# A two-layer decoder trunk: the second layer's input scaling and the low parts of keys and queries, moved from VectorE to GpSimd

## The chip, the core and the metric

The kernel runs on one core of a Trainium2 chip. The time is device microseconds for one execution; the kernel before has a median of 788.73 us in three runs (788.3 to 789.17). In the profile PE is TensorE (PEld its weight loads), DVE is VectorE, ACT is ScalarE, POOL is GpSimd and SP issues most of the DMAs. A line such as L573 is a line of the kernel before, unless the text says otherwise; in the changed kernel the lines from 850 on have a number one higher.

## What is computed

There are 528 tokens (16 meta tokens and 512 of input), width 1024, and two layers. In each, one projection of the normed residual feeds a pooling mixer and a latent attention with eight heads, and gates join the two:

```python
h = rmsnorm(h_res, norm_gain[l])
proj = h @ w_in[l]
u_pool, z_pool, c_q, c_kv, k_rope, z_mla, g_pool, g_mla = jnp.split(proj, IN_SPLIT_POINTS, axis=-1)
y_pool = (pool_mix(u_pool, pool_w_group[l], pool_scale[l]) * jax.nn.silu(z_pool)) @ pool_w_up[l]
...
q = rmsnorm(q, g_qn)
k = rmsnorm(k, g_kn)
...
o = causal_block_attention(q, k, v)
...
merged = jax.nn.sigmoid(g_pool) * y_pool + jax.nn.sigmoid(g_mla) * y_mla
h_res = h_res + merged @ w_out[l]
```

## The kernel before

**Split products.** Every float32 product is made of three matmuls on rounded parts (`mm3`, L188, L191, L192): high weight by high input, high weight by low input, low weight by high input. A part pair comes from two steps: ScalarE copies the value into the rounded type (hi), and VectorE subtracts that from the value (lo). For weights the steps are L183 (`whi`) and L184 (`wlo`), 263 times; for data `split` (L295, L296).

**A stream and its fillers.** All projections form one list of weight chunks of 512 columns, and a generator issues them one after the other. The attention takes steps of that stream to fill the time between its own matmuls (`fill_now`, `fill`, `fill_to`). The framework then orders each engine's instructions by its own timeline of the program, so the order in the code is not quite the order on an engine.

**Layer 2 around the change.** After the query statistics (`qk_stats`) the loop over `renorm` scales the eight input tiles by the norm factor, `inv`, and by the gain, and splits them into `hh` and `hl`; tiles 4 to 7 come first, then 0 to 3, and tiles 0 to 3 are loaded again (L571). Each product is held behind a matmul of the stream. On the same VectorE queue run the Newton steps for the query norm (L303 to L309) and the sums and differences of `mixed` (L583 to L586). Meanwhile PE runs `pu`, which does not need the renormed input; `zm0` and `zm1` behind it are the first that do.

**The heads.** `prep(h)` makes head h's keys and queries: keys times a factor, one half on VectorE (L847), the other on GpSimd (L848), then the parts `kh` and `kl`; queries into `qh` and `ql` (L854, L855), with rotary rows by DMA (L858). Two heads' parts are held at once. `head(h)` makes the scores `S`, the masked extremes (L877), the exponentials (L884), and on GpSimd the products with the reciprocal sums (L922, L924, eight for a head). `prep(h + 1)` follows `head(h)` in the code.

Of the kernel before, what the change touches and what calls it, by code (L numbers as in the profile page):

```python
# [9 lines left out]
F32 = mybir.dt.float32  # L10
# [3 lines left out]
AF = mybir.ActivationFunctionType  # L14
ALU = mybir.AluOpType
# [7 lines left out]
NM = 16  # L23
T = SEQ + NM
# [25 lines left out]
G_H, G_CKV, G_CQ, G_QN, G_QR, G_KN, G_KR, G_PS = 0, 8, 10, 16, 17, 18, 19, 20  # L50
# [22 lines left out]
def trunk(ctx, tc, xT, pos, win, wkr, wqb, wkb, wvb, wgr, wpu, wmu, wout, gains, const, yT):  # L73
    nc = tc.nc
    pe, act, dve, gp, sp = nc.tensor, nc.scalar, nc.vector, nc.gpsimd, nc.sync
# [15 lines left out]
    def slot(tag, dt=F32, bufs=1, w=W):  # L91
        return sl.tile([P, w], dt, tag=tag, name=nm(tag), bufs=bufs)

    def tmp(w=W):
        return tp.tile([P, w], F32, tag="tmp", name=nm("tmp"), bufs=3)
# [104 lines left out]
    newest = [None]  # L200
# [90 lines left out]
        while clk[0] < end and step():  # L291
            pass

    def split(hi, lo, src, a, b):
        act.activation(hi[:, a:b], src, AF.Copy)  # L295
        dve.tensor_sub(lo[:, a:b], src, hi[:, a:b].bitcast(F32))  # L296

    def behind(ins, other):
        tc.add_manual_dep(ins.ins, other.ins.name,
                          mybir.DependencyInfo(mybir.DependencyClass.Sync, mybir.DependencyReason.DATA))  # L300
# [56 lines left out]
    class Layer:  # L357
# [208 lines left out]
        def renorm(self, k):  # L566
            assert k < 4 or (self.l, f"pu{k}") not in done
            f = self.f[k] = slot("sv", bufs=2) if k % 4 == 3 else slot(f"cq{k}")
            f, (hh, hl), x = f[:, NM:T], self.hs[k], xb[:, k, NM:T]
            if k < 4:  # L570
                sp.dma_start(f, scr[:, k, :])  # L571
                x = f
            behind(dve.scalar_tensor_tensor(out=f, in0=x, scalar=self.g(G_H + k), in1=self.inv[:, NM:T],  # L573
                                            op0=ALU.mult, op1=ALU.mult), newest[0])
            split(hh, hl, f, NM, T)

        def mixed(self, i):
            k, s = divmod(i, 2)
            if k > 3 or not self.last:
                return  # L580
            u, w = self.f[k], self.f[k + 4]
            if s == 0:
                dve.tensor_sub(w[:, b:c], u[:, b:c], w[:, b:c])  # L583
                dve.tensor_sub(u[:, b:c], u[:, a:b], u[:, b:c])
                dve.tensor_sub(u[:, a:b], u[:, a:b], w[:, b:c])
                dve.tensor_sub(w[:, a:b], w[:, a:b], u[:, a:b])  # L586
                return
            if k == 0:
                self.half = [sqt().bitcast(F32R) for _ in range(14)]
                spare = slot("rinv", F32R)  # L590
                self.half += [spare[:, 0:HALF], spare[:, HALF:T]]
            th, tl = (slot(f"cq{(3, 0, 1, 2)[k] + j}", F32R) for j in (0, 4))
            t3h, t3l, t4h, t4l = (t[:, :N2] for t in self.half[4 * k:4 * k + 4])
            split(th, tl, u[:, a:c], a, c)
            for h_, l_, v in ((t3h, t3l, w[:, b:c]), (t4h, t4l, w[:, a:b])):
                split(h_, l_, v, 0, N2)
            self.tt[k] = {6: (th[:, a:b], tl[:, a:b]), 5: (th[:, b:c], tl[:, b:c]), 7: (t3h, t3l), 4: (t4h, t4l)}
# [242 lines left out]
        def prep(self, h):  # L840
            p, odd = h // 2, h % 2
            n0, r0 = (64, 0) if odd else (0, 64)
            kf = tmp()
            bc = self.bcs.pop(h)
            if h + 2 < H:
                self.spread_k(h + 2)
            dve.tensor_mul(kf[n0:n0 + 64, :], self.kn[p][n0:n0 + 64, :], bc[n0:n0 + 64, :])  # L847
            gp.tensor_mul(kf[r0:r0 + 64, :], self.kp[r0:r0 + 64, :], bc[r0:r0 + 64, :])  # L848
            kh, kl = slot("kh", F32R, bufs=2), slot("kl", F32R, bufs=2)
            split(kh, kl, kf[:, :T], 0, T)  # L850
            qh, ql = qhl[odd]
            x0 = self.x0
            src = self.qn[p][n0:n0 + 64, x0:T]
            act.activation(qh[n0:n0 + 64, x0:T], src, AF.Copy)  # L854
            dve.tensor_sub(ql[n0:n0 + 64, x0:T], src, qh[n0:n0 + 64, x0:T].bitcast(F32))  # L855
            g0 = 32 * (h % 4)
            for d, f in zip((qh, ql), self.qr[h // 4]):
                sp.dma_start(d[r0:r0 + 32, x0:T].bitcast(F32), f[g0:g0 + 32, x0:T].bitcast(F32))  # L858
            return kh, kl, qh, ql
# [433 lines left out]
```

## Time and profile before

| | |
|---|---|
| median of three runs | 788.73 us |
| the profiled execution | 788.28 us |
| its span | 786.4 us |
| PE busy | 778.8 us |
| DVE busy | 558.8 us |
| ACT busy | 427.1 us |
| POOL busy | 210.9 us |

PE's ends are modelled and its matmuls overlap, so a busy PE may still lose a little; the starts of two matmuls show it better. The groups give a line, engine, operation, the tiles, the shapes and the count, then the busy time, the mean in ns, and the idle time just before with what ended it. Timeline rows give the start, the duration, and the same names. Rows of stretches give busy time by engine.

### The profile page before, as it was taken

How to read it: one execution, taken by the hardware profiler on the slowest of the kernel's cores; microseconds unless marked ns; L12 is line 12 of the kernel's file. 1: busy time of each engine (PE TensorE's matmuls, PEld its weight loads, DVE VectorE, ACT ScalarE, POOL GpSimd, SP SyncE). 2: the span in 40 equal slices, each digit the busy share in tenths (PEclk: the TensorE clock that was granted, in tenths of full speed). 3: DMA queues.
4: the chain of work that ended last, by engine and by line, in shares of the span. 5: the costliest groups of instructions: out<-in, count | busy, mean ns of one | idle time of the engine just before them, and what ended most of it. 6: DMA issues, size and time to landing. Idle time of an engine off the chain costs nothing.

```text
span 786.4 us, 15094 instructions
## 1 busy us (share of the span) xinstructions
PE 778.8 (99%) x5445; PEld 713.4 (91%) x5445; DVE 558.8 (71%) x1229; ACT 427.1 (54%) x974; POOL 210.9 (27%) x275
## 2 busy tenths in 40 slices
PE   9999999999999999999999999999999999999998
PEld 8999899999999999999997898887778999887887
DVE  5848778447788977685355487775897899874932
ACT  8545655635656665643354455556657676654421
POOL 1034504002434342153000145122004323440600
PEclk9999999999999999999999999999999999999999
DMA  6242343434645435647742422435233454462372
GB/s 243 82 101 84 99 120 102 128 106 117 136 122 126 116 90 112 167 103 176 206 141 81 109 81 79 138 97 167 95 111 112 118 153 126 121 202 68 99 231 100
DMA packets 60907, 97.61 MB, mean 124 GB/s; under 512 B 9744, under 2 KB 18320, under 8 KB 60832
## 3 DMA queue, kind: packets, MB, share of 16 engines
q1 hardware_dynamic: 57520, 90.61, 38.8%
q0 software_dynamic: 2304, 4.20, 4.3%
q10 hardware_dynamic: 1008, 1.84, 0.7%
q8 instruction: 43, 0.70, 0.4%
q14 instruction: 32, 0.26, 0.1%
HBM read 88.64 MB, written 14.23 MB: 131 GB/s over the span
## 4 chain that ended last, share of the span: by engine, by line
PE 91%; DVE 4%; DMA 2%; issue 1%; ACT 1%; ACTq 0%; DVEq 0%
PE mm L188 27%; PE mm L192 27%; PE mm L191 26%; PE mm L944 2%; PE S L191 2%; PE S L192 2%; PE S L188 1%; DVE wlo L184 1%; PE o L950 1%; PE o L949 1%; PE S L498 1%; PE mm L400 1%; DMA xb<-xT 1%; DMA raw<-win 1%; DVE hl L296 0%
## 5 line engine op out<-in xcount | busy, mean ns | idle before, releaser
L188 PE MATMUL mm<-hh,whi 128*128 128x264 f32 (+2 forms) x1080 | 333.9, 311 | 0.1
L191 PE MATMUL mm<-hl,whi 128*128 128x264 f32 (+2 forms) x1080 | 332.5, 309 | 0.4 <-DVE hl L296 0.4
L192 PE MATMUL mm<-hh,wlo 128*128 128x264 f32 (+2 forms) x1080 | 332.1, 310 | 0.4 <-DVE wlo L184 0.4
L184 DVE TENSOR_TENSOR wlo<-raw,whi 128x512 fp32r<-128x512 f32 (+2 forms) x263 | 197.7, 756 | 108.8 <-ACT whi L183 105.3
L183 ACT ACTIVATE whi<-raw 128x512 fp32r<-128x512 f32 (+2 forms) x263 | 157.8, 603 | 179.3 <-PE mm L191 114.6
L188 PEld LDWEIGHTS mm<-hh,whi 128*128 128x128 f32 x1080 | 202.9, 188 | 11.8 <-ACT racc L958 0.5
L191 PEld LDWEIGHTS mm<-hl,whi 128*128 128x128 f32 x1080 | 203.3, 188 | 11.1 <-DVE hl L296 0.9
L192 PEld LDWEIGHTS mm<-hh,wlo 128*128 128x128 f32 x1080 | 202.5, 188 | 10.5 <-DVE wlo L184 1.1
L700 POOL TENSOR_TENSOR racc<-racc,tmp 128x264 f32<-128x264 f32 (+1 forms) x15 | 14.2, 950 | 144.2 <-ACT tmp L699 119.8
L192 PE MATMUL mm<-cq,wlo 128*128 128x264 f32 (+2 forms) x140 | 43.5, 313 | 0.6 <-DVE wlo L184 0.6
L188 PE MATMUL mm<-cq,whi 128*128 128x264 f32 (+2 forms) x140 | 44.0, 314 | 0.0
L191 PE MATMUL mm<-cq,whi 128*128 128x264 f32 (+2 forms) x140 | 43.4, 311 | 0.0
L848 POOL TENSOR_TENSOR tmp<-kp,bc 64x528 f32<-64x528 f32 x16 | 23.7, 1484 | 68.5 <-PE mm L815 44.4
L1049 POOL TENSOR_TENSOR tmp<-tmp,xb 128x264 f32<-128x264 f32 (+1 forms) x24 | 27.2, 1155 | 50.4 <-DVE tmp L1047 38.9
L877 DVE CUSTOM_DVE_ANT_0 S<-S,maskw,nqs 128x288 f32<-128x288 f32 (+4 forms) x80 | 38.3, 497 | 3.0 <-PE S L192 2.8
L922 POOL TENSOR_TENSOR pm<-pa,rs 128x16 f32<-128x16 f32 x32 | 10.9, 340 | 96.7 <-DVE rs L917 88.6
L188 PE MATMUL mm<-u,whi 128*128 128x264 f32 (+1 forms) x108 | 35.2, 326 | 0.1
L296 DVE TENSOR_TENSOR tl<-mm,th 128x512 fp32r<-128x512 f32 (+1 forms) x64 | 29.4, 481 | 7.7 <-ACT th L295 6.5
L192 PE MATMUL mm<-u,wlo 128*128 128x264 f32 (+1 forms) x108 | 34.7, 322 | 0.0
L924 POOL TENSOR_TENSOR cq<-cq,rs 128x384 f32<-128x384 f32 (+1 forms) x32 | 32.8, 1024 | 0.0
L191 PE MATMUL mm<-kn,whi 128*128 128x264 f32 (+1 forms) x96 | 30.6, 320 | 0.0
L188 PE MATMUL mm<-q,whi 128*128 128x264 f32 (+1 forms) x96 | 29.9, 323 | 0.6 <-ACT q L295 0.4
(309 smaller groups left out, 1472.3 us busy)
## 6 DMA issues: line engine op xcount, KB each, us to landing
raw<-win SPq DMA_DIRECT2D x139, 256.0 KB, 2.7
raw<-wout SPq DMA_DIRECT2D x32, 256.0 KB, 3.3
bc<-kdr SPq DMA_DIRECT2D x16, 264.0 KB, 4.1
raw<-wpu SPq DMA_DIRECT2D x16, 256.0 KB, 2.8
wsum<-win SPq DMA_DIRECT2D x16, 256.0 KB, 3.3
raw<-wmu SPq DMA_DIRECT2D x16, 256.0 KB, 2.8
raw<-wsum SPq DMA_DIRECT2D x16, 256.0 KB, 3.2
raw<-wqb SPq DMA_DIRECT2D x12, 256.0 KB, 2.6
```

The source lines that it names most:

```text
L183: act.activation(hi[:, :n], raw[:, :n], AF.Copy)
L184: dve.tensor_sub(lo[:, :n], raw[:, :n], hi[:, :n].bitcast(F32))
L188: first = pe.matmul(out, wh, xh, start=start, stop=False, skip_group_check=more)
L191: pe.matmul(out, wh, xl, start=False, stop=False, skip_group_check=more)
L192: newest[0] = pe.matmul(out, wl, xh, start=False, stop=stop, skip_group_check=more)
L296: dve.tensor_sub(lo[:, a:b], src, hi[:, a:b].bitcast(F32))
L700: self.acc_last = gp.tensor_add(self.acc[:, a:b], self.acc[:, a:b], t[:, :b - a])
L848: gp.tensor_mul(kf[r0:r0 + 64, :], self.kp[r0:r0 + 64, :], bc[r0:r0 + 64, :])
L877: dve.tensor_tensor_reduce(out=sv, in0=sv, in1=mask, scale=nqs[:, i, h:h + 1], scalar=3e38, op0=ALU.add, op1=ALU.min, accum_out=bia[:, c:c ...
L924: gp.tensor_mul(pt[i][:, NM:], pt[i][:, NM:], rs[:, i:i + 1].to_broadcast([P, n - NM]))
L944: pe.transpose(tr[:, P * (i - j):P * (i - j + 1)], pt[i][:, NM + P * j:NM + P * (j + 1)], ident)
L1049: gp.tensor_add(t[:, :b - a], t[:, :b - a], self.am[m][:, a:b])
```

## The change

In layer 2 `renorm` multiplies the tile by `inv` on GpSimd, and a ScalarE pass in place applies the gain; before, one VectorE instruction did both. In `prep`, the subtractions that make `kl` and `ql` run on GpSimd in layer 2 and on VectorE in layer 1 as before. Nothing else is changed, and the result is the same quantity.

```diff
-    def split(hi, lo, src, a, b):
+    def split(hi, lo, src, a, b, eng=dve):
         act.activation(hi[:, a:b], src, AF.Copy)
-        dve.tensor_sub(lo[:, a:b], src, hi[:, a:b].bitcast(F32))
+        eng.tensor_sub(lo[:, a:b], src, hi[:, a:b].bitcast(F32))
...
-            behind(dve.scalar_tensor_tensor(out=f, in0=x, scalar=self.g(G_H + k), in1=self.inv[:, NM:T],
-                                            op0=ALU.mult, op1=ALU.mult), newest[0])
+            behind(gp.tensor_mul(f, x, self.inv[:, NM:T]), newest[0])
+            act.activation(f, f, AF.Copy, scale=self.g(G_H + k))
             split(hh, hl, f, NM, T)
...
-            split(kh, kl, kf[:, :T], 0, T)
+            rest = gp if self.last else dve
+            split(kh, kl, kf[:, :T], 0, T, rest)
...
-            dve.tensor_sub(ql[n0:n0 + 64, x0:T], src, qh[n0:n0 + 64, x0:T].bitcast(F32))
+            rest.tensor_sub(ql[n0:n0 + 64, x0:T], src, qh[n0:n0 + 64, x0:T].bitcast(F32))
```

The framework orders each engine anew. GpSimd in layer 2, from the last rotary step of the queries on, in the kernel before (`kp` is the keys' rotary part, `pm` and `pa` belong to head 0's softmax):

```order
L533 TENSOR_TENSOR q_1328_7177<-q_1328_7177,tmp_7183 128x512
L848 TENSOR_TENSOR tmp_7574<-kp_6423,bc_6912 64x528
L848 TENSOR_TENSOR tmp_7761<-kp_6423,bc_6914 64x528
L922 TENSOR_TENSOR pm_7706<-pa_7613,rs_7617 128x16
L924 TENSOR_TENSOR pa_7613<-pa_7613,rs_7617 128x128
```

The same place behind the change (L856 makes ql, L296 kl, L573 the renorm's products; `cq`, `sv` are the renormed tiles, 4 to 7 and then 0 to 3):

```order
L856 TENSOR_TENSOR qhl_106<-q_1339_7221,qhl_105 64x512
L856 TENSOR_TENSOR qhl_108<-q_1339_7221,qhl_107 64x512
L848 TENSOR_TENSOR tmp_7582<-kp_6423,bc_6912 64x528
L573 TENSOR_TENSOR cq_1390_7438<-xb,rinv_6066 128x512
L296 TENSOR_TENSOR kl_7588<-tmp_7582,kh_7587 128x528
L573 TENSOR_TENSOR cq_1395_7463<-xb,rinv_6066 128x512
L573 TENSOR_TENSOR cq_1396_7475<-xb,rinv_6066 128x512
L573 TENSOR_TENSOR sv_7493<-xb,rinv_6066 128x512
L573 TENSOR_TENSOR cq_1402_7505<-cq_1402_7505,rinv_6066 128x512
L573 TENSOR_TENSOR cq_1407_7524<-cq_1407_7524,rinv_6066 128x512
L573 TENSOR_TENSOR cq_1412_7550<-cq_1412_7550,rinv_6066 128x512
L573 TENSOR_TENSOR sv_7563<-sv_7563,rinv_6066 128x512
```

Two products for keys have become twelve operations before the second of them: two ql, kf0, eight renorm products and head 0's kl, which is second among these nine.

VectorE in the renorm stretch before, up to the hl of tile 2 (`hl_11_133`), the last rows of 34 from the first L573:

```order
L573 SCALAR_TENSOR_TENSOR cq_1412_7544<-cq_1412_7544,gn,rinv_6066 128x512
L296 TENSOR_TENSOR hl_9_131<-cq_1407_7519,hh_8_130 128x512
L296 TENSOR_TENSOR sq_7739<-cq_1390_7438,sq_7738 128x256
L584 TENSOR_TENSOR cq_1402_7501<-cq_1402_7501 128x256
L308 TENSOR_TENSOR nt_7419<-nt_7419,na_7417 128x40
L573 SCALAR_TENSOR_TENSOR sv_7556<-sv_7556,gn,rinv_6066 128x512
L184 TENSOR_TENSOR wlo_7597<-raw_7594,whi_7596 128x512
L583 TENSOR_TENSOR cq_1396_7473<-cq_1412_7544,cq_1396_7473 128x256
L584 TENSOR_TENSOR cq_1407_7519<-cq_1407_7519 128x256
L296 TENSOR_TENSOR hl_11_133<-cq_1412_7544,hh_10_132 128x512
```

Behind the change, the last rows of 38 from the first weight split of that stretch to the same hl:

```order
L296 TENSOR_TENSOR hl_9_131<-cq_1407_7524,hh_8_130 128x512
L184 TENSOR_TENSOR wlo_7605<-raw_7602,whi_7604 128x512
L585 TENSOR_TENSOR cq_1402_7505<-cq_1402_7505,cq_1390_7438 128x256
L584 TENSOR_TENSOR cq_1407_7524<-cq_1407_7524 128x256
L583 TENSOR_TENSOR cq_1396_7475<-cq_1412_7550,cq_1396_7475 128x256
L586 TENSOR_TENSOR cq_1390_7438<-cq_1390_7438,cq_1402_7505 128x256
L583 TENSOR_TENSOR sv_7493<-sv_7563,sv_7493 128x256
L585 TENSOR_TENSOR cq_1407_7524<-cq_1407_7524,cq_1395_7463 128x256
L184 TENSOR_TENSOR wlo_7645<-raw_7642,whi_7644 128x512
L296 TENSOR_TENSOR hl_11_133<-cq_1412_7550,hh_10_132 128x512
```

The L573 rows are gone; more of the sums (L583, L585, L586) and a second weight split (`wlo_7645`) stand ahead of this hl, and the whole Newton chain, of which five rows stood ahead of it, is done before them.

GpSimd at head 5 before (`tmp_8700` is its key product, the L922 and L924 rows head 4's softmax):

```order
L848 TENSOR_TENSOR tmp_8700<-kp_6423,bc_8171 64x528
L922 TENSOR_TENSOR pm_8635<-pa_8483,rs_8487 128x16
L924 TENSOR_TENSOR pa_8483<-pa_8483,rs_8487 128x128
...
L924 TENSOR_TENSOR cq_1637_8485<-cq_1637_8485,rs_8487 128x512
L922 TENSOR_TENSOR pm_8635<-pa_8750,rs_8754 128x16
```

Behind the change:

```order
L856 TENSOR_TENSOR qhl_106<-q_1369_7332,qhl_105 64x512
L848 TENSOR_TENSOR tmp_8708<-kp_6423,bc_8179 64x528
L923 TENSOR_TENSOR pm_8643<-pa_8491,rs_8495 128x16
...
L925 TENSOR_TENSOR cq_1637_8493<-cq_1637_8493,rs_8495 128x512
L296 TENSOR_TENSOR kl_8714<-tmp_8708,kh_8713 128x528
L856 TENSOR_TENSOR qhl_108<-q_1369_7332,qhl_107 64x512
L923 TENSOR_TENSOR pm_8643<-pa_8758,rs_8762 128x16
```

Head 5's kl (`kl_8714`) now stands behind all eight of head 4's softmax products; head 2's stands so behind head 1's.

## The prediction

> **What bounds the kernel now.** I read the page first, then the busy time by stretch, then the waits of the matmul engine, then the instructions of the stretch the change touches.
>
> ```profile
> span 786.4 us, 15094 instructions
> PE 778.8 (99%) x5445; PEld 713.4 (91%) x5445; DVE 558.8 (71%) x1229; ACT 427.1 (54%) x974; POOL 210.9 (27%) x275
> PE 91%; DVE 4%; DMA 2%; issue 1%; ACT 1%; ACTq 0%; DVEq 0%
> ```
>
> The matmul engine is busy nearly always and holds 91% of the chain that ended last. A change beside it can win only what it waits for now, and loses whatever new wait it makes. The change lies in layer 2 only: the renorm stretch (about 553 to 575 us) and the eight heads (575 to 690 us).
>
> ```profile
> 550.00:575.00 25.00, 24.15 (x124) 18.06 (x120) 22.89 (x49) 14.18 (x28) 1.52 (x1) 1.00 0.31 96
> 575.00:600.00 25.00, 25.00 (x124) 21.11 (x123) 23.03 (x61) 15.95 (x40) 5.56 (x9) 1.00 0.34 106
> 600.00:690.00 90.00, 89.10 (x620) 82.17 (x620) 81.25 (x197) 64.03 (x167) 33.43 (x51) 1.00 0.43 127
> PE mm L192 <- DVE wlo L184: 1.0, 2, 0.6
> PE o L949 <- DVE tmp L965: 0.5, 1, 0.5
> PE mm L191 <- DVE hl L296: 0.4, 1, 0.4
> PE mm L188 <- DVE sv L625: 0.3, 1, 0.3
> ```
>
> The columns are stretch, its length, then PE, PEld, DVE, ACT, POOL. VectorE is all but full here (22.89 of 25, 23.03 of 25, 81.25 of 90 us), GpSimd nearly empty. The four lower rows are all that PE waits for between 520 and 700 us: 2.2 us, every one ended by VectorE. That is the most that relieving VectorE can be worth by this view.
>
> ```profile
> 568.69 0.40 PE L188 MATMUL mm<-hh,whi 128*128 128x512 f32 x1
> 568.92 0.40 PE L191 MATMUL mm<-hl,whi 128*128 128x512 f32 x1
> 570.55 0.40 PE L191 MATMUL mm<-hl,whi 128*128 128x512 f32 x1
> 571.37 0.50 PE L191 MATMUL mm<-hl,whi 128*128 128x512 f32 x1 [0.43 <-DVE hl L296]
> 571.93 0.40 PE L188 MATMUL mm<-hh,whi 128*128 128x512 f32 x1
> 572.75 0.50 PE L192 MATMUL mm<-hh,wlo 128*128 128x512 f32 x1 [0.42 <-DVE wlo L184]
> ```
>
> At 568.69 the first product with the renormed input (zm0) starts. One matmul of 512 columns starts 0.23 us after the last; the two starts at 571.37 and 572.75 come 0.82 us after theirs, so PE loses 0.59 us twice, 1.2 us in all. PE has caught up with the renorm here, and whatever delays the low parts hl delays the whole kernel.
>
> **The price of an operation on GpSimd.**
>
> ```profile
> L848 POOL TENSOR_TENSOR tmp<-kp,bc 64x528 f32<-64x528 f32 x16 | 23.7, 1484 | 68.5 <-PE mm L815 44.4 <-issue 14.5 <-DVE rs L916 6.5
> L1049 POOL TENSOR_TENSOR tmp<-tmp,xb 128x512 f32<-128x512 f32 x8 | 12.3, 1564 | 34.3 <-DVE tmp L1047 34.3
> L700 POOL TENSOR_TENSOR racc<-racc,tmp 128x512 f32<-128x512 f32 x5 | 6.5, 1293 | 95.0 <-ACT tmp L699 95.0
> L659 POOL TENSOR_TENSOR q<-tmp 128x528 f32<-128x528 f32 x2 | 2.4, 1204 | 0.1
> L296 DVE TENSOR_TENSOR kl<-tmp,kh 128x528 fp32r<-128x528 f32 x16 | 11.3, 704 | 3.0 <-ACT kh L295 3.0
> ```
>
> No GpSimd row has the new operations, but the same shape stands in L700: 1.29 us for 128x512, against 0.70 us for kl on VectorE. The ends are 1.20 (L659, one tile read twice) and 1.56 us (L1049, with waits inside). I take 1.29 for the eight renorm products and the ql, and 1.32 for a kl, the same price at 528 columns.
>
> GpSimd and VectorE do not run beside each other:
>
> ```profile
> 558.33 1.52 POOL L848 TENSOR_TENSOR tmp<-kp,bc 64x528 f32<-64x528 f32 x1 [23.36 <-PE mm L815]
> 558.57 1.83 DVE L184 TENSOR_TENSOR wlo<-raw,whi 128x512 fp32r<-128x512 f32 x1
> 531.87 1.35 POOL L533 TENSOR_TENSOR q<-q,tmp 128x512 f32<-128x512 f32 x1
> 533.30 1.67 POOL L848 TENSOR_TENSOR tmp<-kp,bc 64x528 f32<-64x528 f32 x1
> 532.00 1.77 DVE L296 TENSOR_TENSOR q<-q,q 128x512 fp32r<-128x512 f32 x1
> 533.69 1.82 DVE L184 TENSOR_TENSOR wlo<-raw,whi 128x512 fp32r<-128x512 f32 x1
> ```
>
> The weight split at 558.57 takes 1.83 us, where the kl above takes 0.70: it ends at 560.40, 0.55 us after the GpSimd product that began before it ends (559.85). The same at 532.00 (ends 533.77, GpSimd's at 533.22) and at 533.69 (ends 535.51, GpSimd's at 534.97): 0.55 and 0.54 us after. So a VectorE operation on two SBUF tensors that meets a running GpSimd product stands still until that ends, and GpSimd's next takes longer in turn (1.67 us). The two engines are one queue for such work: a step moved from the one to the other is not taken off that queue; it comes back about twice as long.
>
> [...]
>
> **Term 1, the renorm: +4.0 us.** Per input tile (eight) the change takes a scalar_tensor_tensor off VectorE and adds a GpSimd product and a ScalarE scaling. The low part of head 0's keys moves to GpSimd too, second in its queue.
>
> ```profile
> 552.98 0.73 DVE L573 SCALAR_TENSOR_TENSOR cq<-xb,gn,rinv 128x512 f32<-128x512 f32 x1
> 555.91 0.75 DVE L573 SCALAR_TENSOR_TENSOR cq<-xb,gn,rinv 128x512 f32<-128x512 f32 x1 [0.57 <-PE mm L192]
> 556.58 0.69 DVE L296 TENSOR_TENSOR hl<-cq,hh 128x512 fp32r<-128x512 f32 x1
> 563.23 0.17 DVE L304 TENSOR_SCALAR ny<-ny 128x40 int32<-128x40 int32 x1
> 563.32 0.17 DVE L305 TENSOR_SCALAR na<-na 128x40 f32<-128x40 f32 x1
> 570.31 0.41 DVE L584 TENSOR_TENSOR cq<-cq 128x256 f32<-128x256 f32 x1
> 570.64 0.67 DVE L296 TENSOR_TENSOR hl<-cq,hh 128x512 fp32r<-128x512 f32 x1
> 571.25 0.40 DVE L585 TENSOR_TENSOR cq<-cq,cq 128x256 f32<-128x256 f32 x1
> ```
>
> Start-to-start gives what each costs on a full VectorE: 0.67 us for L573, 0.61 for a 512-wide subtraction, 0.33 for a 256-wide one, 0.1 for a small Newton step. From 552.98 to the end of the hl at 570.64 (tile 2, the one PE waits for at 571.37) before has 34 rows. They come to 8 x 0.67 + 13 x 0.61 + 6 x 0.33 + 7 x 0.1 = 16.0 us; with 0.57 idle before 555.91 and 1.15 of blocking at 558.57 that is 17.7 of the measured 18.3 us (571.31 - 552.98). The sum works.
>
> In the changed order 38 VectorE rows stand from the first weight split to the same hl: 13 of 512 columns, 10 of 256, 15 small ones, 13 x 0.61 + 10 x 0.33 + 15 x 0.1 = 12.7 us. More of Newton and of the sums after it now stands ahead of that hl. GpSimd's nine come to 8 x 1.29 + 1.32 = 11.6 us, all ahead of it too, since a sum on tile 3's product stands before this hl on VectorE. One queue: 24.3 us, so hl of tile 2 ends at 552.98 + 24.3 = 577.3. In the new matmul order its first use stands 14 matmuls after zm0's first: 568.69 + 14 x 0.23 = 571.9. PE loses 5.4 us where it lost 1.2: +4.2. (Tile 3's hl follows three VectorE rows, 1.55 us, later and is used 6 matmuls, 1.4 us, later: nothing more.) GpSimd's product at 533.30 had the queue from 533.77 and ended at 534.97, 1.20 us, a little under the 1.29 taken, so I take +4.0. Ends: GpSimd at 1.56 adds 8 x 0.27 = 2.2, so +6.4; did nothing block, the 1.2 us would go, so -1.2.
>
> ```profile
> 555.14 0.62 ACT L295 ACTIVATE hh<-cq 128x512 fp32r<-128x512 f32 x1
> ```
>
> ScalarE's eight scalings, priced by this copy, are 8 x 0.62 = 5.0 us in a stretch where it is busy 14.18 of 25 us: 19.2 of 25, covered by the longer wait. Were that cover gone, ScalarE would be next: one scaling and one copy per tile, 1.2 us after the last product. The load of tile 3 on the SP queue now stands one weight load later; its product is eighth on GpSimd, so nothing waits for it.
>
> **Term 2, the first two heads' queries: +0.6 us.** Both ql now stand ahead of kf0 on GpSimd, at 533.22, where before had kf0 alone. Alternating: VectorE to 533.77, ql0 to 535.06, weight split to 535.6 (as now), ql1 to 536.9, VectorE to 537.5, kf0 to 538.8, next weight split (256 columns) to 539.1. PE reaches that one 12 matmuls after 535.6, at 538.4. So 0.7 us at most, nothing at least; I take 0.6.
>
> **Term 3, the heads: +1.4 us.** Each head gives GpSimd a kl and a ql, 2.6 us, and takes 2 x 0.61 = 1.2 from VectorE: 1.4 us net on the common queue per head, while VectorE's idle time is 8.75 of 90 us, 1.3 per head. It goes full, and what is late is the keys: kl of heads 2 and 5 now stands behind the softmax products of the head before.
>
> ```profile
> 650.04 0.22 POOL L922 TENSOR_TENSOR pm<-pa,rs 128x16 f32<-128x16 f32 x1 [1.65 <-DVE rs L917]
> 654.18 1.04 POOL L924 TENSOR_TENSOR cq<-cq,rs 128x512 f32<-128x512 f32 x1
> 651.27 0.71 DVE L296 TENSOR_TENSOR kl<-tmp,kh 128x528 fp32r<-128x528 f32 x1
> 654.63 0.34 PE L188 MATMUL S<-kh,qhl 128*128 128x272 f32 x1
> ```
>
> Head 5: the products run from 650.04 to 655.22, kl after them to 656.5; the scores, at 654.63 now, stand some 1.2 us of matmuls later in the new order, 655.9. So 0.6 us is lost there, less or nothing in the others. Two or three such waits make 1.4. Ends: -1.0, if the relieved VectorE ends the waits on L965 and L625 (0.5 + 0.3) and others stay hidden; +6, one us in six heads.
>
> **Sum.** 4.0 + 0.6 + 1.4 = +6.0 us. The profiled execution took 788.28 us (span 786.4 and 1.88 around it); the median of the runs is 0.45 above it, so 788.73 + 6.0 = **794.7 us**.
>
> **Rivals.** (1) *VectorE is relieved and that decides.* VectorE is full where the change takes 8 x (0.67 + 0.61 + 0.61) = 15 us off it, and all four waits of PE are on VectorE: 788.73 - 2.2 = 786.5 us. It needs the GpSimd work to lie where VectorE runs steps that do not block; the 1.83 us split speaks against. [...] 13%. (2) *Both cancel*, PE's 1.2 us at 571 absorbing a shorter delay: 788.7 us within 1.6. 10%. (3) *The heads decide.* If the softmax sums come a microsecond or two later, because VectorE is now full, each key behind them is that late too and seven heads lose 1 to 1.5 us each on top of term 1: 788.73 + 4.6 + 7 to 10 = 800 to 803 us. It decides once the last softmax product of a head ends less than 1.3 us before the next scores. 15%. (4) The forecast, 62%: its own range is 791 to 798.5 us.
>
> **How the numbers follow.** A measurement of this kernel tells about 0.2%, 1.6 us, from no change. Faster is rival 1, 0.13; the same is rival 2, 0.10; slower is the forecast and rival 3, 0.77. The range runs from 787.6, which takes in nearly all of rival 2, to 801, a third of rival 3: left out are 0.13, 0.01 and 0.05 or so.
>
> **What would show it.** Right: PE waits of 2 to 5 us in all at the end of pu7 and the start of zm0, ended by hl L296 and wlo L184; VectorE subtractions of 1.2 to 1.8 us beside the L573 products on GpSimd; the first scores about 4 us later than 575.20 is now, and the later heads no more than 2 us further behind. Wrong: GpSimd products of 1.3 us with VectorE at 0.7 beside them; zm0's start at 568.7 or earlier; or scores that fall behind by a microsecond per head, which is rival 3.

## The result and the profile after

The changed kernel takes 793.39 us (median of 6 runs, 791.93 to 795.05) against 788.95 us for the one before in the same runs: a ratio of 1.0053, 95% interval [1.0033, 1.0073]. Its profiled execution took 791.93 us, 3.65 us above that of before.

The page of the changed kernel: span, busy time by engine, and the chain that ended last.

```profile
span 790.1 us, 15110 instructions
PE 779.0 (99%) x5445; PEld 713.1 (90%) x5445; DVE 560.6 (71%) x1205; ACT 431.3 (55%) x982; POOL 244.9 (31%) x299
PE 88%; DVE 7%; DMA 2%; issue 2%; ACT 1%; POOL 1%; SPq 0%; DVEq 0%; ACTq 0%; POOLq 0%
```

VectorE has 24 instructions fewer, and yet is busy longer (560.6 for 558.8 us). GpSimd has 34 us more. What left VectorE came back to it as standing time, and its share of the chain rose from 4% to 7%.

What PE waits for between 520 and 705 us, the same view that came to 2.2 us before:

```profile
PE mm L192 <- DVE wlo L184: 4.4, 4, 1.6
PE mm L191 <- DVE hl L296: 0.6, 2, 0.3
PE S L188 <- ACT cq L885: 0.2, 1, 0.2
```

PE in the renorm stretch, by start (the matmuls between run 0.23 us apart):

```profile
566.35 0.40 PE L191 MATMUL mm<-th,whi 128*128 128x512 f32 x1
568.40 0.50 PE L192 MATMUL mm<-u,wlo 128*128 128x512 f32 x1 [1.65 <-DVE wlo L184]
...
574.04 0.50 PE L188 MATMUL mm<-hh,whi 128*128 128x512 f32 x1
576.04 0.50 PE L192 MATMUL mm<-hh,wlo 128*128 128x512 f32 x1 [1.50 <-DVE wlo L184]
576.61 0.39 PE L191 MATMUL mm<-hl,whi 128*128 128x512 f32 x1
...
579.16 0.28 PE L188 MATMUL S<-kh,qhl 128*128 128x272 f32 x1
```

From 566.35 to 568.40 PE loses 1.82 us, from 574.04 to 576.04 it loses 1.77; three losses of 0.49, 0.48 and 0.19 lie between. That is 4.75 us where before lost 1.2, and the first scores start at 579.16 instead of 575.20.

GpSimd and VectorE there:

```profile
564.99 1.58 POOL L573 TENSOR_TENSOR cq<-cq,rinv 128x512 f32<-128x512 f32 x1 [1.42 <-PE mm L192]
566.54 1.25 POOL L573 TENSOR_TENSOR sv<-sv,rinv 128x512 f32<-128x512 f32 x1
565.33 1.31 DVE L309 SCALAR_TENSOR_TENSOR ny<-nt,ny 128x40 f32<-128x40 f32 x1
566.56 1.79 DVE L184 TENSOR_TENSOR wlo<-raw,whi 128x512 fp32r<-128x512 f32 x1
575.30 0.68 DVE L184 TENSOR_TENSOR wlo<-raw,whi 128x512 fp32r<-128x512 f32 x1
575.90 0.68 DVE L296 TENSOR_TENSOR hl<-cq,hh 128x512 fp32r<-128x512 f32 x1
```

The weight split that PE waits for at 568.40 starts at 566.56, inside the last product, and ends at 568.35, 0.56 us after that product (567.79). A step of 40 columns (L309), 0.18 to 0.20 us where nothing runs beside it, takes 1.31. GpSimd is done at 567.79, but VectorE is behind until the hl of tile 2, which ends at 576.58; PE takes that hl at 576.61.

### The profile page after: what moved, and what is told of

It reads as the page before. It is cut to its first block, busy times and chain, and to the rows that moved or that the text cites. A ratio compares the mean times of both kernels' runs of the same rounds, so it can differ in the third digit from the quotient of the medians.

```text
span 790.1 us, 15110 instructions
## 1 busy us (share of the span) xinstructions
PE 779.0 (99%) x5445; PEld 713.1 (90%) x5445; DVE 560.6 (71%) x1205; ACT 431.3 (55%) x982; POOL 244.9 (31%) x299
## 4 chain that ended last, share of the span: by engine, by line
PE 88%; DVE 7%; DMA 2%; issue 2%; ACT 1%; POOL 1%; SPq 0%; DVEq 0%; ACTq 0%; POOLq 0%
PE mm L188 26%; PE mm L192 26%; PE mm L191 26%; DVE wlo L184 2%; PE mm L945 2%; PE S L191 1%; PE S L188 1%; PE S L192 1%; PE o L951 1%; PE o L950 1%; PE S L498 1%; DVE S L878 1%; ACT whi L183 1%; PE mm L400 1%; DMA raw<-win 1%
## 5 line engine op out<-in xcount | busy, mean ns | idle before, releaser
L184 DVE TENSOR_TENSOR wlo<-raw,whi 128x512 fp32r<-128x512 f32 (+2 forms) x263 | 201.5, 771 | 112.3 <-ACT whi L183 108.5
L700 POOL TENSOR_TENSOR racc<-racc,tmp 128x264 f32<-128x264 f32 (+1 forms) x15 | 14.3, 950 | 143.8 <-ACT tmp L699 119.8
L878 DVE CUSTOM_DVE_ANT_0 S<-S,maskw,nqs 128x240 f32<-128x240 f32 (+4 forms) x80 | 38.5, 498 | 4.3 <-PE S L192 4.0
L296 DVE TENSOR_TENSOR tl<-mm,th 128x512 fp32r<-128x512 f32 (+1 forms) x64 | 29.6, 482 | 6.4 <-ACT th L295 6.2
L885 ACT ACTIVATE cq<-S,bia 128x400 f32<-128x400 f32 (+2 forms) x48 | 24.5, 515 | 15.0 <-DVE bia L878 8.3
L925 POOL TENSOR_TENSOR cq<-cq,rs 128x384 f32<-128x384 f32 (+1 forms) x32 | 32.3, 1010 | 0.0
```

Of the source, the lines that this page charges most:

```text
L184: dve.tensor_sub(lo[:, :n], raw[:, :n], hi[:, :n].bitcast(F32))
L296: eng.tensor_sub(lo[:, a:b], src, hi[:, a:b].bitcast(F32))
L878: dve.tensor_tensor_reduce(out=sv, in0=sv, in1=mask, scale=nqs[:, i, h:h + 1], scalar=3e38, op0=ALU.add, op1=ALU.min, accum_out=bia[:, c:c ...
L885: act.activation(pv, sv, AF.Exp, scale=-1.0, bias=bia[:, i:i + 1], accum_out=rs[:, c:c + 1])
L925: gp.tensor_mul(pt[i][:, NM:], pt[i][:, NM:], rs[:, i:i + 1].to_broadcast([P, n - NM]))
```

## The experiments

Each was timed in turn with the kernel before, whose median moved from 787.4 to 789.2 us between the groups; so the differences are those within a group. Differences in the text are between medians; the ratios weigh every execution, and one of the six with idle operations in the heads took 800.55 us, which lifts that ratio. The last two columns are PE's lost time, worked out from the starts of successive matmuls: in the renorm stretch (564 to 590 us) and behind 590 us, in the heads.

| kernel | us | before | ratio, 95% | lost in stretch | lost in heads |
|---|---|---|---|---|---|
| before | | | | 1.2 | 2.2 |
| the change | 793.39 | 788.95 | 1.0053 [1.0033, 1.0073] | 4.75 | 1.8 |
| renorm only | 794.42 | 787.92 | 1.0080 [1.0068, 1.0093] | 8.0 | 1.8 |
| keys, queries only | 791.69 | 787.92 | 1.0049 [1.0036, 1.0061] | 0.1 | 5.7 |
| gain on ScalarE only | 789.08 | 787.92 | 1.0021 [1.0012, 1.0031] | 1.1 | 3.1 |
| idle products in the stretch | 798.77 | 787.92 | 1.0143 [1.0127, 1.0158] | 10.3 | 2.2 |
| two heads' parts | 788.98 | 788.03 | 1.0006 [0.9990, 1.0022] | 1.2 | 2.6 |
| one kl | 788.09 | 788.03 | 1.0005 [0.9982, 1.0028] | 1.2 | 1.7 |
| renorm, two heads' parts | 795.56 | 788.03 | 1.0086 [1.0061, 1.0111] | 5.9 | 4.0 |
| half the renorm | 791.38 | 788.03 | 1.0035 [1.0019, 1.0052] | 2.7 | 1.9 |
| keys, queries but head 3's keys | 788.28 | 787.37 | 1.0012 [1.0003, 1.0020] | 0.1 | 2.9 |
| idle operations in the heads | 793.65 | 787.37 | 1.0097 [1.0070, 1.0123] | 1.2 | 7.8 |
| late queries only | 788.65 | 787.37 | 1.0018 [1.0009, 1.0026] | 0.1 | 3.7 |
| one product held | 788.11 | 789.16 | 0.9992 [0.9968, 1.0017] | 0.3 | 1.7 |

The framework orders all engines anew for nearly every edit. Only with one kl, with the idle operations in the heads (nearly) and with one product held does PE keep before's order.

### Which part costs: the renorm alone, and the keys and queries alone

```diff
-            rest = gp if self.last else dve          # renorm only
+            rest = dve
```

> Only the renorm is moved (GpSimd product and ScalarE gain for the eight tiles); kl and ql stay on VectorE. If VectorE and GpSimd are one queue in the renorm stretch, this alone brings most of the cost: the changed kernel loses 4.75 us of PE between 564 and 576 us where the one before loses 1.2, and one GpSimd step of nine (head 0's kl, 1.32 us for 0.61 us) is gone, so +2.5 to +3.8 us: 791.5 to 793 us. If the keys and queries of the heads are what costs, it stays within 1 us of before: 788.5 to 790 us.

```diff
-            behind(gp.tensor_mul(f, x, self.inv[:, NM:T]), newest[0])      # keys, queries only
-            act.activation(f, f, AF.Copy, scale=self.g(G_H + k))
+            behind(dve.scalar_tensor_tensor(out=f, in0=x, scalar=self.g(G_H + k), in1=self.inv[:, NM:T],
+                                            op0=ALU.mult, op1=ALU.mult), newest[0])
```

> Only kl and ql are moved; the renorm is as before. One queue with slack in the heads: +0.3 to +1 us (the wait before the first heads' keys, and head 0's kl in the full renorm stretch), 789.2 to 790 us. If each head loses 0.5 us or more to GpSimd's 2.6 us for VectorE's 1.2 us: +3 us or more, 792 us up. The prediction's own term for the heads would make it +1.4 and +0.6: 791 us.

The renorm alone costs 6.5 us, the parts alone 3.8 us: the renorm alone is dearer than either expectation had it, the parts alone fall under the dearer one (+3 us or more), and the two come to 10.3 us where the whole change costs 4.4. So the costs do not add, and each has something that the whole has not.

In the renorm alone it is mainly TensorE's clock. Stretches of that kernel (the column after POOL is the granted clock), and PE's rows:

```profile
565.00:570.00 5.00, 4.13 (x17) 2.73 (x15) 4.93 (x8) 0.75 (x3) 3.93 (x3) 1.00 0.14 52
570.00:575.00 5.00, 1.20 (x4) 0.60 (x4) 5.00 (x13) 4.73 (x10) 0.00 (x0) 0.89 0.30 90
575.00:580.00 5.00, 5.00 (x12) 3.94 (x13) 5.00 (x13) 2.71 (x7) 0.00 (x0) 0.50 0.18 68
569.02 0.40 PE L188 MATMUL mm<-hh,whi 128*128 128x512 f32 x1
571.67 0.50 PE L191 MATMUL mm<-hl,whi 128*128 128x512 f32 x1 [2.25 <-DVE hl L296]
572.25 0.51 PE L188 MATMUL mm<-hh,whi 128*128 128x512 f32 x1
574.88 0.80 PE L191 MATMUL mm<-hl,whi 128*128 128x512 f32 x1 [2.13 <-DVE hl L296]
```

Two waits of 2.4 us stand 0.6 us apart; then the clock is 0.50, and a dozen matmuls start 0.43 us apart instead of 0.23. Of the 8.0 us lost here some 5.7 are waits and 2.3 the slow clock. Without the clock it would be 1.2 us before against 5.7, +4.5. The 5.7 is still 1.0 more than the change's 4.75. That is about one GpSimd product: head 1's key product runs here right behind the renorm's (567.65 us, 1.33 us long), and in the change only at 588.36. That this product makes the 1.0 us is argued, since the orders differ. In the whole change nearly the same VectorE delay falls mainly in two pieces 6 us apart, and its granted clock stays at 1.00.

In the parts alone it is GpSimd's own queue. GpSimd at head 3, in the kernel with keys and queries only:

```profile
614.14 1.04 POOL L925 TENSOR_TENSOR cq<-cq,rs 128x512 f32<-128x512 f32 x1
615.14 1.30 POOL L848 TENSOR_TENSOR tmp<-kp,bc 64x528 f32<-64x528 f32 x1
617.17 0.70 PE L188 MATMUL S<-kh,qhl 128*128 128x272 f32 x3 [1.33 <-ACT kh L295]
617.19 1.31 POOL L296 TENSOR_TENSOR kl<-tmp,kh 128x528 fp32r<-128x528 f32 x1 [0.75 <-ACT kh L295]
618.56 0.39 PE L191 MATMUL S<-kl,qhl 128*128 128x272 f32 x1 [0.69 <-POOL kl L296]
```

Head 3's key product stands behind head 2's softmax products (L925), its kl behind that, and the scores wait for both. In the change the order is another one:

```profile
611.10 1.31 POOL L848 TENSOR_TENSOR tmp<-kp,bc 64x528 f32<-64x528 f32 x1
614.99 1.33 POOL L296 TENSOR_TENSOR kl<-tmp,kh 128x528 fp32r<-128x528 f32 x1 [2.58 <-ACT kh L295]
618.84 1.29 POOL L856 TENSOR_TENSOR qhl<-q,qhl 64x512 fp32r<-64x512 f32 x1 [2.52 <-ACT qhl L855]
620.68 0.86 POOL L925 TENSOR_TENSOR pa<-pa,rs 128x128 f32<-128x128 f32 x1
```

There head 3's keys are done before head 2's softmax products begin, and no scores wait.

```diff
-            gp.tensor_mul(kf[r0:r0 + 64, :], self.kp[r0:r0 + 64, :], bc[r0:r0 + 64, :])   # and kl likewise
+            (dve if self.last and h == 3 else gp).tensor_mul(kf[r0:r0 + 64, :], self.kp[r0:r0 + 64, :], bc[r0:r0 + 64, :])
```

> Keys' and queries' low parts moved as in the run without the renorm's move, but head 3's keys are made on VectorE altogether (both product halves and kl), so nothing of them stands behind head 2's softmax products on GpSimd. If that queue cost the 3.3 us of PE at 615 to 630 us: 787.8 to 789.2 us, level with before. If the blocking of VectorE by 2.6 us of GpSimd work in each head costs it: still +2.5 to +3.5 us, 790.5 us up.

With head 3's keys off that queue, 2.9 of the 3.8 us are gone, while seven heads' kl and all ql still run on GpSimd. That speaks for the queue and against the price of 2.6 us in each head; PE's order is new in this kernel too, so a part of it may be the order, and a part the clock: between 600 and 625 us it was 0.93 on average with keys and queries only, 1.00 in the kernel before.

### Is it the blocking, or the extra pass on ScalarE?

The blocking is short for what the prediction's rows show: VectorE's steps on SBUF tensors stood still while a GpSimd product ran (the weight split at 558.57 took 1.83 us; the one at 575.30 in the change, with nothing beside it, 0.68), and the other way round (GpSimd's product at 533.30 took 1.67 us; the L700 products 1.29).

```diff
-            behind(gp.tensor_mul(f, x, self.inv[:, NM:T]), newest[0])     # gain on ScalarE only (kl, ql on dve too)
+            behind(dve.tensor_mul(f, x, self.inv[:, NM:T]), newest[0])
```

> The renorm's product stays on VectorE as a plain product of two tiles, and ScalarE applies the gain in place, as in the change; kl and ql stay on VectorE. So it has the change's extra ScalarE pass (eight of some 0.62 us, one more hop before hi and lo) without its GpSimd products. If the cost is the queue that VectorE and GpSimd share: 788.5 to 789.8 us (VectorE saves 8 x 0.06 = 0.5 us, the order puts about that much more ahead of tile 2's low part). If the extra pass and its hop make the delay: +3 to +4 us, 792 to 793 us.

```diff
+            behind(gp.tensor_mul(hl[:, NM:T], x, self.inv[:, NM:T]), newest[0])   # before, and idle products
             behind(dve.scalar_tensor_tensor(out=f, in0=x, scalar=self.g(G_H + k), in1=self.inv[:, NM:T],
```

> Everything is as before, and GpSimd makes eight more products of 128x512 in the renorm stretch, whose results nobody uses (each is written into the low part's tile, which VectorE then overwrites). VectorE's own work is untouched. If a VectorE step on two SBUF tensors stands still while a GpSimd product runs, the eight products come on top: about 7 x 1.25 = 8.8 us ahead of tile 2's low part, and +6 to +9 us, 795 to 798 us, more than the change itself costs. If the engines run beside each other: GpSimd is idle there (1.52 of 25 us), and the time stays at 788.5 to 789.8 us.

The ScalarE pass costs 1.2 us in all and nothing in the stretch (1.1 us lost there, as before); the rest lies in the heads, where the order is new. Eight idle products cost 10.9 us, more than all of the change and more than was expected of them. GpSimd's first row and VectorE's rows in the stretch, with those products:

```profile
554.06 2.62 POOL L573 TENSOR_TENSOR hl<-xb,rinv 128x512 fp32r<-128x512 f32 x1 [17.91 <-issue]
557.15 1.83 DVE L574 SCALAR_TENSOR_TENSOR cq<-xb,gn,rinv 128x512 f32<-128x512 f32 x1
558.90 1.77 DVE L296 TENSOR_TENSOR hl<-cq,hh 128x512 fp32r<-128x512 f32 x1
560.59 1.78 DVE L574 SCALAR_TENSOR_TENSOR cq<-xb,gn,rinv 128x512 f32<-128x512 f32 x1
562.30 1.79 DVE L296 TENSOR_TENSOR hl<-cq,hh 128x512 fp32r<-128x512 f32 x1
```

Steps of 0.67 to 0.73 us take 1.8, one after the other, though none of their inputs comes from GpSimd, and the tile that the hl at 558.90 overwrites was written by 556.68. In these rows the two engines take turns. This kernel too has the clock at 0.50, from 574 to 584 us; some 2.5 of the 10.3 us that PE loses in the stretch are the slow clock, by the starts of its matmuls there (0.43 us apart instead of 0.23).

```diff
+            if k > 3:                                  # half the renorm: tiles 4 to 7
+                behind(gp.tensor_mul(f, x, self.inv[:, NM:T]), newest[0])
+                act.activation(f, f, AF.Copy, scale=self.g(G_H + k))
+            else:
+                behind(dve.scalar_tensor_tensor(...), newest[0])
```

> Half a dose: the renorm of the first four tiles (4 to 7) on GpSimd with ScalarE's gain, of the last four on VectorE as before; kl and ql on VectorE. One common queue: 4 x (1.29 - 0.67) = 2.5 us more before tile 2's low part, less than half of the PE waits of the run with all eight, and no fall of the clock: +1.5 to +2.5 us, 789.5 to 790.5 us. If only the way from product to gain to parts counts (the last tiles' own chain), it is as before: 787.5 to 788.5 us, since PE waits for tiles 0 to 3.

Four tiles cost 3.4 us, eight cost 6.5. The stretch accounts for 1.5 of the 3.4 (2.7 lost for 1.2), as one queue had it; the rest shows in no wait of PE, and the runs of this kernel spread over 4 us.

### One product at a time

```diff
-            split(kh, kl, kf[:, :T], 0, T)             # one kl
+            split(kh, kl, kf[:, :T], 0, T, gp if self.last and h == 0 else dve)
```

> Head 0's kl alone is moved; every matmul keeps its place in before's order. It takes 0.61 us off VectorE at the start of the renorm stretch, where VectorE is full and a product on GpSimd runs anyway. Relief of a full VectorE: PE's 1.2 us at 570 to 572 falls to 0.6 or less, 787.2 to 787.6 us. One common queue: 1.3 us on for 0.6 us off, +0.6 us: 788.2 to 788.7 us.

```diff
-            rest = gp if self.last else dve            # two heads' parts, renorm as before
+            rest = gp if self.last and h < 2 else dve
```

> kl and ql of heads 0 and 1 only are moved; later heads and the renorm are as before. The run that moved all heads' parts lost 0.14 us of PE at 570 to 572 us where before loses 1.2, but 3.3 us more at head 3, whose keys (from 615.14) stood behind head 2's softmax products on GpSimd. If it is that queue that cost it 3.8 us, nothing of it is left: -1.0 + 0.3 (the wait at 537.5), so 0.5 to 1 us below before, 787.0 to 787.9 us. If VectorE's blocking by each kl and ql costs it, two heads of eight keep a quarter: +1 us, 788.5 to 789.2 us.

Neither differs measurably from before, and PE's loss in the stretch stays at 1.2 us in both: VectorE relieved of 0.6 us gains nothing, GpSimd loaded with 1.3 us costs nothing one could see. With one kl, neither of the two expected shifts in the stretch came. VectorE is not full where that kl runs (553.49 to 555.23 us): it idles 0.94 us before a weight split at 554.98 and 0.46 us before the next renorm step at 556.24, which is held behind a matmul. In these two, head 1's key product still runs in the stretch. In three other kernels it stood later by chance of the order, and there PE lost 0.1 us instead of 1.2. So it was held on purpose:

```diff
-            gp.tensor_mul(kf[r0:r0 + 64, :], self.kp[r0:r0 + 64, :], bc[r0:r0 + 64, :])   # one product held
+            kg = gp.tensor_mul(kf[r0:r0 + 64, :], self.kp[r0:r0 + 64, :], bc[r0:r0 + 64, :])
+            if self.last and h == 1:
+                behind(kg, self.s1)                    # s1: the last score matmul on head 0's s2
```

> The kernel before, with one dependency more: GpSimd's key product of head 1 (at 558.33 in before's trace, 1.52 us, the only GpSimd work in the renorm stretch) waits for head 0's score matmuls on s2, so that it runs behind the stretch; no engine's order changes. It blocked one weight split by 1.15 us there, and PE lost 1.2 us at 570 to 572. If one GpSimd product in that stretch costs PE what it blocks: PE's loss there falls to about 0.1 to 0.2 us, and the time to 1.0 us below before, 786.4 to 787 us where before has 787.4 to 788. If the product runs beside VectorE for nothing, PE loses 1.2 us as before, and the time is before's. If the product now blocks a step that PE needs at 577 to 583 us, the gain comes back there.

PE in that kernel, at the place where before lost 0.59 us twice:

```profile
573.64 0.40 PE L188 MATMUL mm<-hh,whi 128*128 128x512 f32 x1
574.01 0.53 PE L192 MATMUL mm<-hh,wlo 128*128 128x512 f32 x1
574.37 0.40 PE L188 MATMUL mm<-hh,whi 128*128 128x512 f32 x1
```

Two losses of 0.14 and 0.13 are left of 1.2 us, with no engine's order changed and this one product moved: so 0.9 of the 1.15 us by which it blocked a weight split were PE's loss there. The time is 1.05 us lower by the medians, but its interval takes in no change; a version that beats the kernel before is not shown.

### The heads

```diff
-            rest = gp if self.last else dve            # the change, without heads 2 to 7
+            rest = gp if self.last and h < 2 else dve
```

> The changed kernel, but heads 2 to 7 keep kl and ql on VectorE: what is missing against the changed kernel is the prediction's term for the heads. By that term (+1.4 us) it is 3.0 us above before: 791 us. If the heads cost nothing there (PE loses some 1.5 us in them after the change, 2.0 before): as the changed kernel, +4 to +5 us, 792 to 793 us. More than that if PE's waits in the renorm stretch come close enough together that the granted clock falls to 0.50, as in the run with the renorm alone (12 matmuls of 512 columns 0.43 us apart instead of 0.23 from 575.29 on): 794 us.

```diff
+            if self.last and h > 1:                    # before, and idle operations in the heads
+                gp.tensor_sub(kf[:, :T], kf[:, :T], kh.bitcast(F32)[:, 0:T])
+                gp.tensor_sub(kf[:, 0:T], kf[:, :T], kh.bitcast(F32)[:, 0:T])
```

> Everything is as before, and in heads 2 to 7 GpSimd makes two more operations of 128x528 whose results nobody uses (in place on the key tile, after kh and kl are taken from it): 2.6 us per head, what kl and ql take there in the change, with VectorE's work untouched. By the prediction's common queue they come on top, 6 x 2.6 = 15.6 us against some 8.75 us of VectorE's idle time in the heads: +4 to +7 us, 792 to 795 us. If most VectorE steps of a head read PSUM and run beside GpSimd (in the run with keys and queries moved, four steps on the scores S took 0.36 to 0.52 us inside or beside GpSimd operations): within 1 us of before, 787.5 to 789 us. A third way is the queue on GpSimd: the next head's softmax products and key product stand behind the idle ones, +1 to +3 us.

```diff
-            rest = gp if self.last else dve            # late queries only: kl and renorm on dve
+            rest = gp if self.last and h > 1 else dve
```

> Only ql of heads 2 to 7 is moved; kl and the renorm stay on VectorE. A head's ql is not behind its keys, so if the queue of the keys on GpSimd was the whole cost of the moved parts, this costs nothing and takes 6 x 0.61 = 3.7 us off VectorE: 787 to 788.3 us. If the order that the framework makes anew moves things by itself: 788.5 to 790.5 us.

The three do not say the same. With the renorm on GpSimd, moving the parts of heads 2 to 7 as well is worth 3.1 us (4.4 above before instead of 7.5); with the renorm on VectorE it costs 2.8 (3.8 instead of 0.95). Of the 3.1 us, 1.15 lie in the renorm stretch and not in the heads: without the later parts on GpSimd, head 1's key product runs right behind the renorm's (568.26 us, 1.78 us long), where the change has it at 588.36. The other 2.2 us lie in the heads. With the order held nearly fixed, the same load on GpSimd, as idle operations, costs 6.3 us. PE's waits in the kernel with those:

```profile
PE mm L188 <- DVE sv L638: 2.1, 1, 2.1
PE mm L192 <- DVE wlo L184: 1.4, 3, 0.6
PE S L188 <- ACT kh L295: 1.3, 1, 1.3
PE mm L947 <- POOL cq L927: 1.2, 1, 1.2
PE mm L188 <- DVE sv L625: 1.0, 1, 1.0
```

Both ways of losing are there: the blocking (VectorE's sv come 2.1 and 1.0 us late) and GpSimd's queue (the keys 1.3, the softmax products 1.2 us late). And the late queries alone, which no scores were found waiting for, still cost 1.3 us: PE loses 1.9 us between the starts at 626.65 and 628.74, for VectorE's tmp (L635), and 0.8 us between 594.73 and 595.61, for a softmax product on GpSimd. So the load is dear in the heads, and how much of it a kernel pays varies with the order that the framework makes.

## Why the prediction was right, and where it was not

**The renorm, +4.0 us.** PE lost 4.75 us for 1.2, +3.6. The hl of tile 2, put at 577.3, ended at 576.58. The mechanism is shown by the idle products (+10.9 us with VectorE's steps unchanged), by the single one held with every engine's order as before, and by ScalarE's pass, which alone cost the stretch nothing. The step of 24.3 us for one queue held: from GpSimd's first product (553.09) to the end of that hl the changed kernel took 23.5 us. What the sum had otherwise: it put the whole loss in one wait, for hl. It came mainly in two pieces, both at weight splits that stand behind that work on VectorE; the prediction's signs, the end of pu7 and wlo beside hl, had named that. The split mattered more than it looks: in the renorm alone nearly the same delay fell in one place, and the clock added 2.3 us. The prediction had no term for that. Nor is the queue made of steps on two SBUF tensors alone, as the last section shows.

**The price.** Taken as 1.29 us for a product and a ql, and 1.32 for a kl. GpSimd's groups in the changed kernel:

```profile
L573 POOL TENSOR_TENSOR cq<-cq,rinv 128x512 f32<-128x512 f32 x3 | 4.2, 1414 | 1.5 <-PE mm L192 1.4
L856 POOL TENSOR_TENSOR qhl<-q,qhl 64x512 fp32r<-64x512 f32 x8 | 11.6, 1453 | 37.0 <-ACT qhl L855 36.8
L296 POOL TENSOR_TENSOR kl<-tmp,kh 128x528 fp32r<-128x528 f32 x8 | 11.2, 1400 | 10.3 <-ACT kh L295 10.3
```

The means of 1.40 to 1.45 us hold time in which GpSimd stood still beside VectorE; single rows have 1.25 to 1.32.

**The first heads' queries, +0.6 us.** A new loss of 0.29 us ahead of the matmul at 538.58 in the change, and nearly the same in every kernel that moved these two ql: about half of what was taken, inside its ends.

**The heads, +1.4 us.** This is the term that was mis-sized: PE loses 1.8 us there where before lost 2.2, so -0.4. The step that failed took the common queue's net time per head, let VectorE go full by it, and let two or three waits come out of it in the order shown. VectorE did not go full: between 600 and 690 us it is busy 80.88 us after the change and 81.25 before, while GpSimd goes from 33.43 to 48.80. (So GpSimd was not nearly empty in the heads before the change, as the prediction had it; its softmax products are the queue that the keys stood in.) Head 5's kl did run behind the softmax products, as forecast, but no wait came of it:

```profile
656.55 1.78 POOL L296 TENSOR_TENSOR kl<-tmp,kh 128x528 fp32r<-128x528 f32 x1
659.68 0.29 PE L191 MATMUL S<-kl,qhl 128*128 128x272 f32 x1
```

It ended at 658.33. The prediction had the scores wait for it. They do start before, at 655.05, but with products that read kh alone, and the first that reads kl starts at 659.68, 1.35 us after kl is there. Head 3's keys, too, stand ahead of the softmax products in the change. A load on GpSimd as such is not cheap (the idle operations cost 6.3 us). That the work taken off VectorE also ended waits is argued: with the renorm and only two heads' parts moved PE lost 4.0 us in the heads, but in another order.

**The sum.** 3.6 + 0.3 - 0.4 = 3.5 us against 3.65 between the profiled executions and 4.4 between the medians; forecast were 6.0. Of the 2.5 us that it was too high by, 1.8 are the heads' term. All three terms were too high, so none made up for another; but the medians lie 0.9 us further apart than the rows account for, and that much of the forecast's closeness is luck.

**The rivals.** VectorE is relieved: no, its busy time rose. Both cancel: no, PE lost 3.6 us more than before at 564 to 576 us. The heads decide, 1 to 1.5 us in each: not in this kernel, but its mechanism, a key behind the softmax products, goes with the 2.9 us at one head in the run with keys and queries only. It stays open why the framework's order puts it so in one kernel and not in the other.

## What to carry to other kernels

Where VectorE was full and made what PE needed next, GpSimd was no second engine for work on two SBUF tensors: a product there cost a full VectorE nearly its whole length (0.7 us off, 1.3 us on), and even one such product in the wrong stretch cost PE 0.9 us. Where VectorE idled (0.94 and 0.46 us beside the one kl), it cost nothing that the runs show (ratio 1.0005). Count both engines as one queue up to the step PE waits for, then look whether the waits stand close together, because in the renorm alone the clock added half as much again (2.3 us on 4.5). Behind that step, ask when PE first reads what is late: not every late step makes a wait. And where a scheduler makes the order, the parts of a change measured alone need not add up to the change: compare kernels whose order is the same, or say how much the order moves (here PE lost 1.7 to 4.0 us in the heads of kernels that left heads 2 to 7 on the engines of before and added nothing there).

## What was not expected of the hardware

*GpSimd starved as well.* In the kernel with one product held, that product took 6.43 us instead of 1.3. GpSimd's row, and VectorE's beside it:

```profile
577.94 6.43 POOL L848 TENSOR_TENSOR tmp<-kp,bc 64x528 f32<-64x528 f32 x1 [40.57 <-PE S L192]
578.00 0.41 DVE L585 TENSOR_TENSOR sv<-sv,sv 128x256 f32<-128x256 f32 x1
...
582.49 0.67 DVE L296 TENSOR_TENSOR cq<-cq,cq 128x512 fp32r<-128x512 f32 x1
583.09 0.67 DVE L562 SCALAR_TENSOR_TENSOR u<-tmp,mm 128x512 f32<-128x512 f32 x1
583.68 1.23 DVE L184 TENSOR_TENSOR wlo<-raw,whi 128x512 fp32r<-128x512 f32 x1
```

From 578.00 on VectorE runs back to back on SBUF tensors at their usual lengths, and GpSimd does not get in. At 583.09 comes a step whose second input, mm, is in PSUM. The product ends at 584.37, 1.28 us after that start, and the next split, at 583.68, ends 0.54 us after the product. So the 6.43 us are waiting and running, and the end fits a start at the one step with a PSUM input. That this input let GpSimd in is the author's reading of one place. In the kernel with keys and queries only, VectorE's tl (L296), made from mm in PSUM, took 0.42 us at 607.33, beside GpSimd's ql (606.48 to 607.78), and 0.41 at 618.97 with no GpSimd work beside it; four steps on the scores S, in PSUM too, took 0.36 to 0.52 us inside or beside GpSimd operations.

*Some one-input steps stood still too.* In the changed kernel, beside one of the renorm's products:

```profile
559.43 1.43 POOL L573 TENSOR_TENSOR sv<-xb,rinv 128x512 f32<-128x512 f32 x1 [0.28 <-PE mm L192]
560.02 0.89 DVE L303 TENSOR_SCALAR ny<-na 128x40 int32<-128x40 int32 x1
```

L303 reads one SBUF tensor. It takes 0.17 us at 561.88 in the kernel before, and here 0.89, ending 0.05 us after GpSimd's product. L304, with one input as well, takes 1.23 at 560.94 in the changed kernel, beside the next product (from 560.83, at most 1.36 us long), and 0.17 at 563.23 in the kernel before. So a step with one SBUF input was no safe neighbour for GpSimd here.

*The clock fell after close waits.* In the renorm-only kernel PE had four matmuls between 569.3 and 574.9 us; the granted clock was 0.50 from 574 to 580, 0.63 in the next microsecond and 1.00 from 581. It fell though no single wait was over 2.4 us, and the fall lasted some 6.8 us; in the changed kernel two waits of 1.8 us, 6 us apart, did not bring it (1.00 from 565 to 590). Nor did losses of 1.64, 0.48, 0.18 and 1.77 us between 571.32 and 577.68 in the kernel with the renorm and two heads' parts. Where between these the limit lies, no run shows.
